# Where the low parts of stationary weights begin: one fixed place, or sixteen places in turn

## The chip, the cores and the metric

The kernel runs on one core of one Trainium2 chip. The metric is the device time of one execution in microseconds (us), as the median of several runs. The profile shows one execution, taken by the hardware profiler. Its engines are PE (TensorE, the matmuls), PEld (TensorE's weight loads), DVE (VectorE), ACT (ScalarE), POOL (GpSimd) and SP (SyncE, which issues most transfers).

## The reference

One decoder layer on 256 tokens of width 2048, in float32. A combined projection feeds a sliding-window attention (16 heads, learned sinks, ALiBi) and a forgetting attention (16 heads, per-head gates); both are normalised and sent through one output projection. Then comes a GeGLU channel mixer of width 5632 with a causal convolution of width 3 between the up-projection and the activation. Every sub-layer is `x + post_norm(f(pre_norm(x)))`:

```python
h = rmsnorm(x, pre_mix_g[l])
proj = h @ w_in[l]
...
mix = jnp.concatenate([o_a, o_b], axis=-1) @ w_out[l]
x = x + rmsnorm(mix, post_mix_g[l])
h = rmsnorm(x, pre_ffn_g[l])
u = causal_dwconv(h @ w_up[l], conv_w[l], conv_b[l])
gate, val = jnp.split(u, 2, axis=-1)
y = (jax.nn.gelu(gate, approximate=True) * val) @ w_down[l]
x = x + rmsnorm(y, post_ffn_g[l])
```

## The kernel before

**Split numbers.** Every matrix product is made of three products of a shorter float format (`float32r`): each operand is split into a high part, which is its rounded value, and a low part, which is the rest. The sum is high x high + high x low + low x high. The split of weights is `w_split` (lines 101 to 117): ScalarE writes the high part (line 111, tile `whi`), VectorE subtracts it from the raw weights and writes the low part (line 114, tile `wlo`). `w_high` (lines 89 to 99) does the same in two steps. A unit of weights is 128 partitions x 1024 numbers (512 KB), loaded by SyncE into `raw` (line 68), with five buffers each for `raw`, `whi` and `wlo`. The tile `wlo` is 128 numbers longer than a unit (line 85), so that a low part can begin later in it; the place is chosen in `w_parts` (lines 76 to 87).

**Two ways to multiply.** In `proj_T` (lines 242 to 269) and in `unit_T` (lines 213 to 240) the weights are the stationary operand, the one that is loaded into the array, and the activations `hT` are the moving operand. These calls hand `still=True` down to `w_parts`. `hT` holds the high part of the activations of 256 tokens in its columns 0 to 255 and the low part in columns 256 to 511, so one matmul of 512 columns with a high weight makes two of the three products (line 252), and one of 256 columns with a low weight makes the third (line 257). In `mm3` (lines 271 to 275), used by the value columns of the input projection, the output projection and the down-projection, activations are stationary and weights are the moving operand; there `still` is false and the low part begins at the start of its tile. `first_gate` (lines 841 to 881) uses `gate_unit` with `still=True` for one group of columns (matmuls at lines 860 and 864).

**Order on TensorE.** `proj_T` makes 256 columns of output from 2048 rows of weights, in two halves (`v` is 0 or 2) of two units each. A half is fifteen high matmuls, sixteen low ones in a row, and the last high one, in the order in which the code stands. Each of these matmuls has its own 128 columns of weights, so a weight load stands before each. TensorE's order is the program's own (line 46: `manual_schedule` for PE). Around the end of the mixer, ScalarE, VectorE and GpSimd have the program's order too (line 743); elsewhere a scheduler sets theirs. `tick` and `later` (lines 54 to 60) put steps of the attention between the matmuls of a projection.

**Stages in time.** Input projection and sliding-window attention come first, then the value columns, then the forgetting attention between further projections, then the output projection, then twice (for each half of the 5632 columns) the up-projection with `proj_T` and the down-projection with `mm3`.

**Memory.** Two unused tiles named `room` (lines 134 and 135) fill up the pools ahead of the others. In the built program the tiles `raw`, `whi`, `wlo`, `hT`, `rest`, `oT` and `G` all begin at multiples of 512 bytes in each partition.

Of the kernel before, what the change touches and what calls it, by code (L numbers as in the profile page):

```python
# [30 lines left out]
def hybrid_layer(ctx: ExitStack, tc: tile.TileContext, x, pre_mix_g, w_in, b_forget, sinks,  # L31
# [39 lines left out]
        return raw, a, c  # L71


    LOW = 80

    def w_parts(n, keep=None, still=False):


        if keep and keep[0] is None:
            return keep[1]  # L80
        if keep:
            return [keep[0].tile([P, UNIT], F32R, tag="h" + x, bufs=keep[1], name="w" + x)[:, :n]
                    for x in ("hi", "lo")]
        hi = wp.tile([P, UNIT], F32R, tag="whi", bufs=WB, name="whi")
        lo = wp.tile([P, UNIT + 128], F32R, tag="wlo", bufs=WB, name="wlo")
        c = LOW if still else 0
        return [hi[:, :n], lo[:, c:c + n]]

    def w_high(unit, keep=None, still=False):

        raw, a, c = unit
        n = a * c
        hi, lo = w_parts(n, keep, still)
        act.copy(hi, raw[:, :n])

        def low():
            dve.tensor_tensor(lo, raw[:, :n], hi.bitcast(F32), op=ALU.subtract)

        return [x.rearrange("p (a c) -> p a c", a=a) for x in (hi, lo)], low

    def w_split(unit, pin=False, keep=None, begun=None, between=None, still=False):

        raw, a, c = unit
        n = a * c
        hi, lo = begun or w_parts(n, keep, still)
        for i in range(2 if between else 1):
            cs = slice(i * 512, i * 512 + 512) if between else slice(0, n)
            if i:
                between()
            if not between or i:  # L110
                i1 = act.copy(hi[:, cs], raw[:, cs])  # L111
                if pin:
                    tc.keep_in_program_order(i1)
            i2 = dve.tensor_tensor(lo[:, cs], raw[:, cs], hi[:, cs].bitcast(F32), op=ALU.subtract)  # L114
            if pin:
                tc.keep_in_program_order(i2)
        return [x.rearrange("p (a c) -> p a c", a=a) for x in (hi, lo)]
# [163 lines left out]
    with tc.tile_pool(name="mixp", bufs=1) as mp:  # L281
# [47 lines left out]


        begun = w_parts(UNIT, still=True)
        tc.keep_in_program_order(dve.tensor_copy(begun[0][:, 0:512], head[:, 0:512]))
        x_part(0, (0,), "acc")
# [461 lines left out]
    with tc.tile_pool(name="ffn", bufs=1) as fp:  # L795
# [198 lines left out]
        for i, n in enumerate((512, 512, 512, 256, 256)):  # L994
            c = (0, 512, 1024, 1536, 1792)[i]
# [30 lines left out]
```

## Time and profile before

| | |
|---|---|
| median of 3 runs | 1082.71 us (1082.71 to 1083.7) |
| profiled execution | 1083.01 us, span 1081.2 us |
| granted TensorE clock | 0.997 |
| PE busy | 1069.4 us, 99% of the span, 6002 matmuls |
| PEld busy | 931.3 us, 86% |
| DVE busy | 735.1 us, 68% |
| ACT busy | 621.7 us, 57% |
| POOL busy | 186.1 us, 17% |
| memory read | 199.58 MB, 187 GB/s over the span |

The span goes from the first to the last instruction; the execution's time is a little longer. Rows of the profile name a line of the code, an engine, an operation, output and input tiles, and how often it occurs. Matmuls are pipelined: a row's duration of one matmul is longer than the distance from its start to the start of the next, so busy time does not tell how densely they follow. The distance is read from starts and counts in the timeline. In the chain of work that ended last, each piece is put down to the engine and line that the next one had to wait for.

### The profile page before, as it was taken

What the parts mean: (1) busy time and instruction counts of PE and PEld (TensorE: products, weight loads), DVE (VectorE), ACT (ScalarE), POOL (GpSimd) and SP (SyncE); (2) the same over time, 40 slices, a digit from 0 to 9 for tenths busy, and PEclk for the clock granted to TensorE, in tenths of its full rate; (3) what the DMA queues carried; (4) which work ended last, traced back from release to release, by engine and by line L of the source; (5) the groups of instructions that cost most, each with busy time, mean ns of one, the idle gap of its engine ahead of it and who ended that gap; (6) DMA issues with size and microseconds to landing.
All of it is one profiled execution on the core that took longest, in us unless ns stands there. A gap on an engine that the chain in (4) does not pass through costs nothing.

```text
span 1081.2 us, 16296 instructions
## 1 busy us (share of the span) xinstructions
PE 1069.4 (99%) x6002; PEld 931.3 (86%) x6002; DVE 735.1 (68%) x1193; ACT 621.7 (57%) x1069; POOL 186.1 (17%) x252
## 2 busy tenths in 40 slices
PE   9999999999999999999999999999999999999996
PEld 7889988888889888888888888888888888888886
DVE  5987877787467876777767444457777677765563
ACT  6766766667556765655556444456565565644450
POOL 4243334442022110101011000001010100101111
PEclk9999999999999999999999999999999999999998
DMA  8645556554863766566566556665665656665552
GB/s 284 205 132 162 175 159 203 167 165 156 291 234 105 233 191 195 182 192 196 184 191 191 194 196 192 195 197 178 192 195 189 190 187 193 189 196 192 192 167 78
DMA packets 164970, 202.88 MB, mean 188 GB/s; under 512 B 6780, under 2 KB 130972, under 8 KB 164380
## 3 DMA queue, kind: packets, MB, share of 16 engines
q1 hardware_dynamic: 164176, 201.27, 58.5%
q8 instruction: 47, 0.77, 0.3%
q10 hardware_dynamic: 716, 0.58, 0.2%
q14 instruction: 31, 0.25, 0.1%
HBM read 199.58 MB, written 2.11 MB: 187 GB/s over the span
## 4 chain that ended last, share of the span: by engine, by line
PE 94%; DVE 2%; POOL 1%; DMA 1%; ACT 1%; issue 0%; SPq 0%; DVEq 0%; POOLq 0%; ACTq 0%
PE bank_acc L275 35%; PE bank_acc L252 22%; PE bank_att L252 14%; PE bank_acc L257 11%; PE bank_att L257 7%; PE bank_att L440 1%; DVE wlo L114 1%; PE bank_att L484 1%; PE bank_att L475 1%; PE bank_att L486 0%; PE bank_att L220 0%; DMA cb<-c_dram 0%; DVE hT L721 0%; DMA x_in<-in_x_dram 0%; ACT whi L111 0%
## 5 line engine op out<-in xcount | busy, mean ns | idle before, releaser
L114 DVE TENSOR_TENSOR wlo<-raw,whi 128x1024 fp32r<-128x1024 f32 (+3 forms) x357 | 452.4, 1269 | 256.8 <-ACT whi L111 179.3
L111 ACT CAST whi<-raw 128x1024 fp32r<-128x1024 f32 (+3 forms) x356 | 368.1, 1036 | 187.4 <-PE bank_acc L275 119.7
L252 PE MATMUL bank_acc<-hT,whi 128*128 128x512 f32 x1088 | 266.6, 392 | 0.0
L252 PEld LDWEIGHTS bank_acc<-hT,whi 128*128 128x128 f32 x1088 | 198.3, 188 | 37.4
L275 PE MATMUL bank_acc<-whi,G 128*128 128x512 f32 (+1 forms) x724 | 214.4, 378 | 0.0
L275 PEld LDWEIGHTS bank_acc<-whi,G 128*128 128x128 f32 x724 | 133.7, 188 | 25.5
L252 PE MATMUL bank_att<-hT,whi 128*128 128x512 f32 x640 | 154.2, 391 | 0.0
L831 POOL TENSOR_TENSOR u<-u,rowf 128x256 f32<-128x256 f32 x88 | 54.4, 640 | 540.1 <-DVE u L830 537.8
L257 PEld LDWEIGHTS bank_acc<-hT,wlo 128*128 128x128 f32 x1088 | 138.5, 189 | 5.7
L257 PE MATMUL bank_acc<-hT,wlo 128*128 128x256 f32 x1088 | 142.2, 282 | 0.0
L252 PEld LDWEIGHTS bank_att<-hT,whi 128*128 128x128 f32 x640 | 117.6, 188 | 22.8
L275 PE MATMUL bank_acc<-wlo,G 128*128 128x512 f32 (+1 forms) x362 | 137.1, 379 | 0.0
L257 PEld LDWEIGHTS bank_att<-hT,wlo 128*128 128x128 f32 x640 | 81.0, 189 | 3.1
L275 PE MATMUL bank_acc<-whi,oT 128*128 128x512 f32 (+1 forms) x272 | 82.4, 380 | 0.0
L257 PE MATMUL bank_att<-hT,wlo 128*128 128x256 f32 x640 | 82.0, 281 | 0.0
L275 PEld LDWEIGHTS bank_acc<-wlo,G 128*128 128x128 f32 x362 | 68.1, 188 | 12.8
L275 PEld LDWEIGHTS bank_acc<-whi,oT 128*128 128x128 f32 x272 | 50.2, 188 | 9.3
L275 PE MATMUL bank_acc<-wlo,oT 128*128 128x512 f32 (+1 forms) x136 | 51.2, 377 | 0.0
L275 PE MATMUL bank_acc<-whi,hT 128*128 128x384 f32 (+1 forms) x192 | 47.5, 323 | 0.0
L829 ACT COPY cs<-bank_acc 128x256 f32<-128x256 f32 x48 | 15.9, 372 | 52.7 <-PE bank_acc L252 52.7
L458 ACT ACTIVATE p<-p,nm 128x256 f32<-128x256 f32 (+1 forms) x64 | 28.4, 444 | 27.7 <-DVE nm L446 27.7
L829 ACT COPY cs<-bank_att 128x256 f32<-128x256 f32 x40 | 13.3, 373 | 47.8 <-PE bank_att L252 47.6
(195 smaller groups left out, 1025.9 us busy)
## 6 DMA issues: line engine op xcount, KB each, us to landing
raw<-in_w_up_dram SPq DMA_DIRECT2D x176, 512.0 KB, 3.8
raw<-in_w_down_dram SPq DMA_DIRECT2D x88, 512.0 KB, 4.7
raw<-in_w_in_dram SPq DMA_DIRECT2D x51, 512.0 KB, 3.4
raw<-in_w_out_dram SPq DMA_DIRECT2D x32, 512.0 KB, 4.1
raw<-in_w_in_dram SPq DMA_DIRECT2D x16, 384.0 KB, 3.4
cb<-c_dram SPq DMA_DIRECT2D x8, 256.0 KB, 4.1
x_sb<-in_x_dram SPq DMA_DIRECT2D x2, 1024.0 KB
raw<-in_w_in_dram SPq DMA_DIRECT2D x5, 408.0 KB, 3.4
```

The source lines that it names most:

```text
L111: i1 = act.copy(hi[:, cs], raw[:, cs])
L114: i2 = dve.tensor_tensor(lo[:, cs], raw[:, cs], hi[:, cs].bitcast(F32), op=ALU.subtract)
L252: pe.matmul(b, parts[u][0][:, a, m * P:(m + 1) * P], hT[:, kt, :], start=(kt == 0), stop=(kt == KT - 1))
L257: pe.matmul(b[:, 256:512], parts[u][1][:, a, m * P:(m + 1) * P], hT[:, (v + u) * 4 + a, 0:256], start=False, stop=False)
L275: pe.matmul(b, a, r[:, cols], start=(first and i == 0), stop=(last and i == 2))
L440: pe.matmul(sb[e][:, cs], a[r, t * P:(t + 1) * P], b[r, 0:nk], start=(n == 0), stop=(n == 2))
L458: act.activation(p[:, e, cs], p[:, e, cs], AF.Exp, bias=nm[:, t, e:e + 1], scale=-1.0, accum_out=rs[:, t, e:e + 1])
L475: pe.transpose(pb[:, i * P:(i + 1) * P], p[:, e, c:c + P], ident)
L484: pe.matmul(ov, values(hl, 0), p[:, :, 0:256], start=(n == 0), stop=False)
L829: act.copy(c, b[:, 256:512])
L831: pool.tensor_tensor(u[:, 2:258], u[:, 2:258], rowf, op=ALU.mult)
```

## The change

The constant `LOW` goes. In its place a counter, `turn_no`, counts the units whose weights are stationary. The low part of such a unit begins at one of sixteen places in its tile, 8 numbers (32 bytes) apart; two units in succession share a place, then the place moves on by five sixteenths. The places in their order are 0, 40, 80, 120, 32, 72, 112, 24, 64, 104, 16, 56, 96, 8, 48 and 88 numbers, and then 0 again. Before, all these units began at 80 numbers. Since the counter is even at the start of each half of `proj_T`, both units of a half share a place. Units with weights as moving operand begin at 0 as before. The tile's size stays.

```diff
-    LOW = 80
+
+    turn_no = [0]
 
     def w_parts(n, keep=None, still=False):
...
         hi = wp.tile([P, UNIT], F32R, tag="whi", bufs=WB, name="whi")
         lo = wp.tile([P, UNIT + 128], F32R, tag="wlo", bufs=WB, name="wlo")
-        c = LOW if still else 0
+        c = turn_no[0] // 2 * 5 % 16 * 8 if still else 0
+        turn_no[0] += still
         return [hi[:, :n], lo[:, c:c + n]]
```

## The prediction

> **What bounds the kernel now.** I read the page first (busy time, then the chain that ended last), then the waits of TensorE, then its timeline and the durations by line, because the change moves no instruction.
>
> ```profile
> PE 1069.4 (99%) x6002; PEld 931.3 (86%) x6002; DVE 735.1 (68%) x1193; ACT 621.7 (57%) x1069; POOL 186.1 (17%) x252
> ...
> PE 94%; DVE 2%; POOL 1%; DMA 1%; ACT 1%; issue 0%; SPq 0%; DVEq 0%; POOLq 0%; ACTq 0%
> PE bank_acc L275 35%; PE bank_acc L252 22%; PE bank_att L252 14%; PE bank_acc L257 11%; PE bank_att L257 7%; PE bank_att L440 1%; DVE wlo L114 1%; PE bank_att L484 1%; PE bank_att L475 1%; PE bank_att L486 0%; PE bank_att L220 0%; DMA cb<-c_dram 0%; DVE hT L721 0%; DMA x_in<-in_x_dram 0%; ACT whi L111 0%
> ```
>
> TensorE is the bound: 94% of the chain is its own work. Line 257 is the pass with the moved operand, a low part as stationary operand: 11% + 7% = 18% of the chain, some 195 us. The waits of TensorE (engine, line, what for; us in total, times, longest) say that it waits for nearly nothing else:
>
> ```profile
> PE bank_acc L168 <- DVE junk L163: 1.3, 1, 1.3
> PE bank_att L630 <- POOL sqs L501: 0.9, 1, 0.9
> PE bank_acc L300 <- DMA x_in<-in_x_dram: 0.4, 1, 0.4
> PE bank_att L208 <- DVE diag L202: 0.4, 1, 0.4
> ```
>
> So the question is the rate at which the matmuls follow each other. The timeline of TensorE in the up-projection (start, length of the merged row, count at the end) shows it; one half of proj_T is one row of each kind:
>
> ```profile
> 463.86 2.05 PE L257 MATMUL bank_att<-hT,wlo 128*128 128x256 f32 x16
> 465.74 3.82 PE L252 MATMUL bank_att<-hT,whi 128*128 128x512 f32 x16
> 469.40 2.05 PE L257 MATMUL bank_att<-hT,wlo 128*128 128x256 f32 x16
> 471.28 3.82 PE L252 MATMUL bank_att<-hT,whi 128*128 128x512 f32 x16
> ```
>
> A row of x16 ends with the whole duration of its last matmul (0.28 us for a low, 0.39 for a high), so a low follows the low before it after (2.05 - 0.28) / 15 = 118.0 ns, and a high after (3.82 - 0.39) / 15 = 228.7 ns. Every load of weights stands between two of them. A matmul of 256 columns takes half of the time of one of 512, so behind a low there is the least time to load the next 128 columns, and a load that is held up shows at once. The same form, 256 columns with new weights each time, runs at two other rates in this trace:
>
> ```profile
> 176.93 1.30 PE L257 MATMUL bank_acc<-hT,wlo 128*128 128x256 f32 x10
> 190.75 1.30 PE L257 MATMUL bank_acc<-hT,wlo 128*128 128x256 f32 x10
> ...
> 1067.86 1.60 PE L275 MATMUL bank_acc<-rest,G 128*128 128x256 f32 x12
> 1069.30 0.28 PE L275 MATMUL bank_acc<-whi,G 128*128 128x256 f32 x1
> ```
>
> The two runs of line 257 in the attention stage go at (1.30 - 0.28) / 9 = 113.3 ns, at the place of today. At the end of the kernel, where the stationary operand is G, twelve go in 1069.30 - 1067.86 = 1.44 us, 120.0 ns each. The tiles of the built program tell the places: hT (and rest, in the same memory), whi, G and oT begin at multiples of 512 bytes; the low parts of proj_T begin 320 bytes past one (LOW = 80 elements), and every 128-column slice of them steps by 512, so the place is the same for all slices. Thus 120.0 ns stands for a place of 0 against a moving operand at 0, and 113.3 or 118.0 for 320 against 0. The modelled durations carry the same steps:
>
> ```profile
> L257 PE MATMUL bank_acc<-hT,wlo x1088: 276/281/386, 36.7 to 950.9; 128*128 128x256 f32 x182
> L257 PE MATMUL bank_att<-hT,wlo x640: 280/281/283, 369.7 to 928.8; 128*128 128x256 f32 x160
> L225 PE MATMUL bank_att<-hT,wlo x32: 280/281/416, 8.2 to 29.7; 128*128 128x256 f32 x32
> L225 PE MATMUL bank_acc<-hT,wlo x32: 276/280/287, 13.2 to 32.5; 128*128 128x256 f32 x32
> L860 PE MATMUL bank_acc<-hT,wlo x48: 223/276/281, 340.1 to 353.9; 128*128 128x128 f32 x32, 128*128 128x256 f32 x16
> L275 PE MATMUL bank_acc<-rest,G 128*128 128x256 f32 x24 | 3.2, 283 | 0.0
> ```
>
> 276 ns belongs to the runs at 113.3, 281 to those at 118, 283 (the last row, a mean) to those at 120. The longest, 287 at line 225, is 11 ns over 276: 113.3 + 11 = 124.3 ns is the slowest rate that the rows support.
>
> **The change, part by part.** Nothing is added or removed: every engine and queue has the same instructions in the same order with the same waits. What moves is the start of the low part: per pair of units it takes 0, 160, 320, 480, 128, 288, 448, 96, 256, 416, 64, 224, 384, 32, 192, 352 bytes and so on, instead of always 320. Of the rows above, 1088 + 640 (line 257) + 64 (line 225) + 48 (line 860) = 1840 matmuls load from it, 115 at each place on average.
>
> *Places that are multiples of 64 bytes* (eight of the sixteen, 920 matmuls). Two have rows: 320 goes at 118.0 ns and 0 at 120.0. For the other six nothing speaks for either end, so I take the middle for all eight, 119.0 ns: 920 x 1.0 ns = +0.9 us. Bounds, if all but 320 fell to one end: 113.3 ns, -4.3 us, and 124.3 ns, +5.8 us.
>
> *Places 32 bytes past a multiple of 64* (the other 920). No operand that TensorE reads here stands so; the trace has no row. The bounds are the same two rates, 113.3 and 124.3 ns, or -4.3 and +5.8 us. I take the middle of today's rate and the slow bound, (118.0 + 124.3) / 2 = 121.2 ns, near the 120.0 of place 0, because a start off the grid on which all else lies can make a load of 512 bytes touch one piece more and, on these rows, can hardly make it shorter than at 320: 920 x 3.2 ns = +2.9 us.
>
> *The high parts behind each run of lows.* Line 252 goes at 228.7 ns, while the same size at line 275 goes at 226.7, three matmuls in 1036.32 - 1035.64 = 0.68 us:
>
> ```profile
> 1035.64 0.61 PE L275 MATMUL bank_acc<-whi,G 128*128 128x512 f32 x2
> 1036.09 0.39 PE L275 MATMUL bank_acc<-wlo,G 128*128 128x512 f32 x1
> 1036.32 0.61 PE L275 MATMUL bank_acc<-whi,G 128*128 128x512 f32 x2
> ```
>
> That is 16 x 2.0 = 32 ns for each of 1728 / 16 = 108 halves, 3.5 us: the highs pay for some matmuls after the lows until loads and matmuls run in step again. A new place could end this (-3.5 us) or double it (+3.5). I take nothing, since both rates of the lows now lead into the same highs.
>
> *VectorE's subtraction (line 114, or 97), which writes the low part.* The same 228 tiles and bytes, only at another start. In the stretch from 370 to 560 us, which is up-projection alone:
>
> ```profile
> L114 DVE TENSOR_TENSOR wlo<-raw,whi 128x1024 fp32r<-128x1024 f32 x69 | 90.3, 1309 | 44.3 <-ACT whi L111 15.8 <-issue 13.8 <-PE bank_acc L257 7.3
> L111 ACT CAST whi<-raw 128x1024 fp32r<-128x1024 f32 x69 | 72.3, 1048 | 17.5 <-PE bank_att L252 9.1 <-PE bank_acc L252 8.4
> ```
>
> One of 1.31 us per unit lies under some 2.77 us of matmuls (half of 471.28 - 465.74), and VectorE sat idle 44.3 us before them in 190. A slowdown by a tenth would be 0.13 us of that; what hides it is VectorE's slack, and were it used up, line 257 would wait for wlo, which the waits of TensorE do not show now. I cost it at nothing. Loads from memory, ScalarE and the buffers' turns keep their order and sizes: nothing.
>
> *Sum*, against the profiled execution: 1083.01 (span 1081.2 and 1.8 around it) + 0.9 + 2.9 = 1086.8 us. The median of the runs is 1082.71, 0.3 below the profiled one; 1086.8 is 0.38% above it. About 0.2%, 2.2 us, is what a measurement of this kernel can tell from no change.
>
> **The rivals.** *Faster: most places are free.* One mechanism: whether a load meets the reads of the running matmul depends on the place, and 320, which is held up by 118.0 - 113.3 = 4.7 ns in nearly all its runs, is one of the bad ones. If 11 of 16 places ran at 113.3 and five at 120.0, the mean would be 115.4 ns, 1840 x -2.6 = -4.8 us, 1078.2 us. It needs more than 30% free places to break even (120.0 - 6.7 f = 118.0), and more than 48% for 0.2% (1.2 ns per matmul). For it: 113.3 occurs with the change's operands. Against: of two places with rows the other one is slower.
>
> *No change: the place does not set the rate.* The rows at 176.93 and 463.86 have one place and two rates, so the moment at which a run begins decides as well; G's 120.0 comes with another moving operand. If that were all, each place would show 118 mostly, and the time would be 1083.0 us. Against: about a hundred runs enter alike, in step, and go at 118.
>
> The Trainium skill has a rule that comes to the same: in "TensorE: Matmul & The Clock Gate", section "Step-by-step: what each phase is for", TensorE has two independent read ports, and loading the next tile's weights takes no read bandwidth from the running matmul. By that the place costs nothing, 1083.0 us; the rows at 113.3, 118.0 and 120.0 ns for one form do not bear it out fully.
>
> *Slower still: the odd places go at the slow bound.* If a start 32 bytes off the grid gave 124.3 ns, with the even ones at 119.0, it is 920 x 6.3 + 920 x 1.0 = +6.7 us, 1089.7 us. For it: all tiles lie on the grid. Against: 287 is the maximum of a row whose median is 280.
>
> **How the numbers follow.** My forecast, slower by about 3.8 us, gets 0.42; the slow bound at the odd places 0.20; no change 0.18; free places 0.20. So slower by over 0.2% is 0.62, within it 0.18, faster 0.20. The forecast's own range is 1084.5 to 1088.5 us (odd places between 118.5 and 123). For 8 in 10 the range reaches into the rivals of both signs, from 1080 to 1091 us: above lies the case of odd places at 124.3 with longer highs behind, below the larger half of the free case.
>
> **What would show it.** Right: the median duration of line 257 rises from 281 towards 283 or more, rows of x16 differ from half to half (above 2.05 us for the places 32 bytes off, the 2.08 of 120.0 ns or more at place 0), a pattern that repeats after sixteen halves; line 252 stays near 228.7 ns; no new wait of TensorE for wlo; line 114 keeps its 1.2 to 1.3 us. Wrong: rows of 1.98 us (113.3 ns) at many places, or all rows at 2.05 as now, or highs that move by more than 1 ns each.

## The result and the profile after

The changed kernel takes 1084.46 us (median of 14 runs, 1083.75 to 1085.82), the kernel before 1082.93 us on the same chip (14 runs, 1081.83 to 1083.7). The ratio is 1.0019, with a 95% interval of 1.0011 to 1.0026: slower by 1.5 us by the medians and 2.1 by the ratio, just under the 0.2% that a measurement can tell, though its interval leaves out no change. The forecast was +3.8 us. The measured median lies 0.04 us below the forecast's own range (1084.5 to 1088.5 us) and inside the range that was to hold in 8 of 10 cases (1080 to 1091 us).

Line 257 of before is line 259 here, line 252 is 254, line 114 is 116. First the waits of TensorE in the changed kernel (engine, line, what for; us in total, times, longest):

```profile
PE bank_acc L170 <- DVE junk L165: 1.3, 1, 1.3
PE bank_att L632 <- POOL sqs L503: 0.9, 1, 0.9
PE bank_att L210 <- DVE diag L204: 0.3, 1, 0.3
PE bank_att L222 <- ACT whi L113: 0.3, 1, 0.3
```

No wait for the low part of a half has come up. Neither has VectorE become slower; its subtraction in the stretch from 370 to 560 us:

```profile
L116 DVE TENSOR_TENSOR wlo<-raw,whi 128x1024 fp32r<-128x1024 f32 x69 | 90.3, 1309 | 45.0 <-ACT whi L113 16.1 <-issue 14.1 <-PE bank_att L259 7.4
```

1309 ns, as before to the nanosecond. The loss is inside the stream of matmuls. The timeline of TensorE in the up-projection shows it (start, length of the merged row, count), here the lows of eight halves in a row:

```profile
408.07 2.05 PE L259 MATMUL bank_acc<-hT,wlo 128*128 128x256 f32 x16
...
413.63 2.05 PE L259 MATMUL bank_att<-hT,wlo 128*128 128x256 f32 x16
415.52 3.85 PE L254 MATMUL bank_att<-hT,whi 128*128 128x512 f32 x16
419.21 2.04 PE L259 MATMUL bank_att<-hT,wlo 128*128 128x256 f32 x16
421.08 3.82 PE L254 MATMUL bank_att<-hT,whi 128*128 128x512 f32 x16
424.74 2.08 PE L259 MATMUL bank_att<-hT,wlo 128*128 128x256 f32 x16
...
430.32 2.08 PE L259 MATMUL bank_att<-hT,wlo 128*128 128x256 f32 x16
432.24 0.62 PE L254 MATMUL bank_att<-hT,whi 128*128 128x512 f32 x2
432.69 3.35 PE L254 MATMUL bank_acc<-hT,whi 128*128 128x512 f32 x14
435.88 2.05 PE L259 MATMUL bank_acc<-hT,wlo 128*128 128x256 f32 x16
...
441.43 2.03 PE L259 MATMUL bank_acc<-hT,wlo 128*128 128x256 f32 x16
...
446.96 2.08 PE L259 MATMUL bank_acc<-hT,wlo 128*128 128x256 f32 x16
```

Where all undisturbed halves of the up-projections took 2.05 us for sixteen lows before, they now take 2.03 to 2.08. By the code, the rows from 408.07 on begin at 288, 448, 96, 256, 416, 64, 224 and 384 bytes. The row at 415.52, highs behind place 448, is 3.85 us long where the others are 3.82: a place shows in the high parts too. The rows at 432.24 and 432.69 show how a half is made: fourteen high matmuls, sixteen low ones and two high ones (not fifteen and one, as the section on the kernel before has it). Where the bank does not change, the last two highs of a half and the first fourteen of the next stand in one row of sixteen.

The starts of the single matmuls in the trace give the cost of each place more finely. It repeats after 256 bytes: 320 costs what 64 does, 448 what 192 does, so there are eight different places. A half is undisturbed where no other matmul stands between its own, as in the up-projections; nearly all of these agree within a nanosecond for one place, though ScalarE, VectorE and the transfers do something else beside each.

| place modulo 256 | last high before the lows, ns | distance of lows, ns | last low and 15 highs behind, ns | sum of a half, ns |
|---|---|---|---|---|
| 0 | 226 | 119.5 | 3547 | 5566 |
| 32 | 235 | 118.3 | 3563 | 5573 |
| 64 (before: 320) | 226 | 117.8 | 3547 | 5540 |
| 96 | 229 | 117.3 | 3545 | 5534 |
| 128 | 233 | 120.4 | 3528 | 5567 |
| 160 | 237 | 119.7 | 3547 | 5580 |
| 192 | 226 | 117.8 | 3581 | 5574 |
| 224 | 235 | 116.8 | 3540 | 5527 |

Each time goes from the start of a matmul to the start of a later one. The sum is the first column, 15 distances of lows, and the third. Its mean is 5558 ns against 5540 ns for the one place of before: 18 ns for each of 108 halves, 1.9 us. The profiled executions agree, by the first and last start of line 257 or 259 (here the row of after; that of before is in the prediction):

```profile
L259 PE MATMUL bank_acc<-hT,wlo x1088: 274/281/388, 35.9 to 951.9; 128*128 128x256 f32 x182
```

From the first to the last low 951.9 - 35.9 = 916.0 us pass, before it was 950.9 - 36.7 = 914.2: 1.8 us more. The whole spans differ by only 1.0 us because this execution reached its first low 0.8 us earlier.

### The profile page after: what moved, and what is told of

The parts are those of the page before. It is cut to its first block, busy times and chain, and to the rows that moved or that the text cites. A ratio compares the mean times of both kernels' runs of the same rounds, so it can differ in the third digit from the quotient of the medians.

```text
span 1082.2 us, 16296 instructions
## 1 busy us (share of the span) xinstructions
PE 1070.2 (99%) x6002; PEld 930.3 (86%) x6002; DVE 735.5 (68%) x1193; ACT 622.0 (57%) x1069; POOL 185.8 (17%) x252
## 4 chain that ended last, share of the span: by engine, by line
PE 93%; DVE 2%; DMA 1%; POOL 1%; ACT 1%; issue 0%; SPq 0%; DVEq 0%; POOLq 0%; ACTq 0%
PE bank_acc L277 35%; PE bank_acc L254 22%; PE bank_att L254 14%; PE bank_acc L259 11%; PE bank_att L259 7%; PE bank_att L442 1%; PE bank_att L486 1%; PE bank_att L477 1%; DVE wlo L116 1%; DMA x_in<-in_x_dram 1%; PE bank_att L488 0%; DMA cb<-c_dram 0%; DVE hT L723 0%; POOL p L534 0%; ACT whi L113 0%
```

## The experiments

Theory 1: each place has a cost of its own, made of the last high before, the lows, and the highs behind, that does not depend on what the place before was. Theory 2, the rival: the places cost alike, and it is the change of place that costs. The first four kernels tell them apart; three keep one place throughout.

**One place, 56 numbers (224 bytes past a multiple of 256).**

```diff
-    LOW = 80
+    LOW = 56
```

> All low parts of stationary weights begin at 56 numbers (224 bytes past a multiple of 256). Theory 1, the costs of a place add up and repeat after 256 bytes: from the trace of the changed kernel, lows at 116.8 ns instead of 117.8 (15 x -1.0 = -15 ns a half), highs behind them 7 ns shorter, last high before the lows 9 ns longer: -13 ns for each of some 114 halves, 1.5 us faster than before. Theory 2, a place costs nothing and the change of place costs: the same as before within 0.3 us.

1081.9 us against 1083.11 before (11 and 23 runs); ratio 0.9990, interval 0.9981 to 0.9998: 1.1 to 1.2 us faster. It is the one kernel of this study with an interval wholly below the kernel before, though by less than 0.2%. A row of its timeline:

```profile
474.80 2.03 PE L257 MATMUL bank_att<-hT,wlo 128*128 128x256 f32 x16
```

2.03 us for sixteen lows, as at 441.43 in the changed kernel. The halves of its up-projections take 5525 to 5528 ns, where the table's sum is 5527.

**One place, 40 numbers (160 bytes).**

```diff
-    LOW = 80
+    LOW = 40
```

> All low parts begin at 40 numbers (160 bytes past a multiple of 256), the place with the longest sum in the changed kernel: lows 119.7 ns, highs as before, last high 10 ns longer. Theory 1: +40 ns a half, some 4.6 us slower than before, slower than the kernel with sixteen places. Theory 2: as before.

1087.15 us against 1083.11 (4 and 23 runs); ratio 1.0040, interval 1.0026 to 1.0054: 4.0 to 4.3 us slower, more than the kernel with sixteen places. Its halves take 5580 ns, the table's sum:

```profile
470.32 2.08 PE L257 MATMUL bank_att<-hT,wlo 128*128 128x256 f32 x16
```

**One place, 48 numbers (192 bytes).**

```diff
-    LOW = 80
+    LOW = 48
```

> All low parts begin at 48 numbers (192 bytes past a multiple of 256). In the changed kernel the lows of this place run at 117.8 ns, as those at 80 numbers do, and the highs behind them take 33 ns more. Theory 1: rows of sixteen lows as before, +34 ns a half in the highs, some 3.9 us slower than before. Theory 2, and also the view that the rate of the lows alone makes the difference: as before.

1086.51 us against 1083.11 (6 and 23 runs); ratio 1.0033, interval 1.0021 to 1.0045, though its lows go as before. Here are the first whole half, in the input projection, and one of the up-projections:

```profile
44.10 1.98 PE L257 MATMUL bank_acc<-hT,wlo 128*128 128x256 f32 x16
...
470.00 2.05 PE L257 MATMUL bank_att<-hT,wlo 128*128 128x256 f32 x16
471.89 3.85 PE L252 MATMUL bank_att<-hT,whi 128*128 128x512 f32 x16
```

In the up-projections the lows' rows are those of before, 2.05 us; the highs' row is 3.85 instead of 3.82, and a half takes 5573 or 5574 ns. So a place is paid for after its lows as well, and one that looks equal by the rate of line 257 costs 3.4 us. The row at 44.10 is an exception: at the same place, behind two highs that follow other work, its sixteen lows go at 113.3 ns.

**Turning between two places that are equal modulo 256.**

```diff
-        c = turn_no[0] // 2 * 5 % 16 * 8 if still else 0
+        c = (80, 16)[turn_no[0] // 2 % 2] if still else 0
```

> The place changes for every two units, but only between 80 and 16 numbers (320 and 64 bytes, both 64 past a multiple of 256). Theory 1: as before within 0.5 us, every half 5.54 us. Theory 2, the change of place costs: some 1.5 us slower, like the kernel with sixteen places.

1082.32 us against 1083.11; ratio 0.9998, interval 0.9989 to 1.0007. Turning by itself costs nothing that shows, and 64 and 320 are the same place: all undisturbed halves of the up-projections take 5539 or 5540 ns. Theory 2 falls with this and with fixed40 and fixed48, which never turn and are slower than the kernel that does.

**The two classes of the prediction's sum, each alone.** The prediction costed the multiples of 64 bytes and the places 32 past one apart.

```diff
-        c = turn_no[0] // 2 * 5 % 16 * 8 if still else 0
+        c = turn_no[0] // 2 * 5 % 8 * 16 if still else 0
```

> Only the eight places that are multiples of 64 bytes, in turn. The prediction's step: lows at 119.0 ns on average, all 1840 of them 1.0 ns over before, +1.8 us, and less than the odd places cost. Theory 1 with the costs by place read from the changed kernel's trace (5566, 5541, 5567 and 5574 ns a half for 0, 64, 128 and 192): +22 ns a half, some +2.5 us, more than the odd places cost.

```diff
-        c = turn_no[0] // 2 * 5 % 16 * 8 if still else 0
+        c = turn_no[0] // 2 * 5 % 8 * 16 + 8 if still else 0
```

> Only the eight places 32 bytes past a multiple of 64, in turn. The prediction's step: lows at 121.2 ns on average, 1840 x 3.2 ns, +5.9 us, three times what the even places cost. Theory 1 (5573, 5534, 5580 and 5527 ns a half for 32, 96, 160 and 224): +14 ns a half, some +1.5 us, less than the even places cost.

Even places: 1084.82 us against 1082.84, ratio 1.0019 (1.0010 to 1.0028). Odd places: 1084.73, ratio 1.0015 (1.0006 to 1.0024). The runs cannot tell the two apart, but the odd ones are far from the +5.9 us of the prediction's step; the even ones fit both its +1.8 and theory 1's +2.5. The mean halves in their traces are 5562 ns for the even and 5553 ns for the odd places, as the table's sums give.

Two runs ask what a place is measured from. Theory 3: from the moving operand, modulo 256. Theory 4: from the start of the memory, the load's place alone.

**Everything 64 bytes further on.**

```diff
-    const.tile([P, 120], F32, tag="room", name="room_c")
+    const.tile([P, 136], F32, tag="room", name="room_c")
```

> The unused tile ahead of all others is 64 bytes longer, so the moving operand hT, the high and the low parts all stand 64 bytes further on; the distances between them stay. Theory 3, what counts is the distance between the load's place and that of the moving operand modulo 256: halves of 5.54 us with lows at 117.8 ns as before. Theory 4, what counts is the load's own place: the low parts now stand at 128 past a multiple of 256, so lows at 120.4 ns as that place has in the kernel with sixteen.

1082.87 us beside 1082.65 for the kernel before, one run each. The halves take 5540 ns, and the lows 2.05 us a row as before, though they now stand at 128:

```profile
474.74 2.05 PE L257 MATMUL bank_att<-hT,wlo 128*128 128x256 f32 x16
```

**The moving operand alone 64 bytes further on.**

```diff
-    LOW = 80
+    LOW = 16
...
-        lo = wp.tile([P, UNIT + 128], F32R, tag="wlo", bufs=WB, name="wlo")
+        lo = wp.tile([P, UNIT + 64], F32R, tag="wlo", bufs=WB, name="wlo")
...
     x_in = main.tile([P, 2, D], F32, tag="x", name="x_in")
+    main.tile([P, 16], F32, tag="ahead", name="ahead")
...
     hT = main.tile([P, KT, 512], F32R, tag="hT", name="hT")
+    main.tile([P, 112], F32, tag="behind", name="behind")
```

> Only the moving operand hT stands 64 bytes further on; high parts stay at 0 and low parts at 64 past a multiple of 256 (16 numbers, in tiles of 1024 + 64 numbers). Theory 3: the lows get the distance 0 and run at 119.5 ns as place 0 does, the highs get a distance that the traces have not shown. Theory 4: lows at 117.8 ns and highs as before.

1087.01 us beside 1082.65, one run each. The lows have not moved modulo 256, and yet they run as place 0 did:

```profile
470.68 2.08 PE L259 MATMUL bank_att<-hT,wlo 128*128 128x256 f32 x16
472.59 3.84 PE L254 MATMUL bank_att<-hT,whi 128*128 128x512 f32 x16
...
741.29 2.08 PE L259 MATMUL bank_att<-hT,wlo 128*128 128x256 f32 x16
```

(2.08 - 0.28) / 15 = 120.0 ns. By the single starts there are two kinds of halves: in the first up-projection all forty undisturbed ones have lows at 120.0 ns and take 5593 or 5594 ns; in the second all forty-three have lows at 119.5 ns, just as place 0 had, and take 5573 or 5574. The addresses are the same in both; why the stream settles in two ways is open. (The whole time also holds the products of `mm3`, in which the shifted memory is an operand too.) Theory 4 falls with both runs; theory 3 stands for the lows. The cost thus depends on the load of the next weights and the reads of the running matmul together; how the two get in each other's way, the profile does not show. The Trainium skill, in "TensorE: Matmul & The Clock Gate", section "Step-by-step: what each phase is for", has these two on independent read ports, so that a load takes nothing from the running matmul. The runs do not bear that out: with the same instructions, and 3.7 us of waits listed for TensorE in each, the distance between the two addresses moves the kernel by 5.25 us (fixed56 to fixed40).

**Other places for the high parts.**

```diff
-        hi = wp.tile([P, UNIT], F32R, tag="whi", bufs=WB, name="whi")
-        lo = wp.tile([P, UNIT + 128], F32R, tag="wlo", bufs=WB, name="wlo")
-        c = turn_no[0] // 2 * 5 % 16 * 8 if still else 0
+        hi = wp.tile([P, UNIT + 64], F32R, tag="whi", bufs=WB, name="whi")
+        lo = wp.tile([P, UNIT + 64], F32R, tag="wlo", bufs=WB, name="wlo")
+        s = turn_no[0] // 2 - 28
+        d, c = (max(s, 0) // 10 % 8 * 8, (s % 10 - 2) % 8 * 8) if still else (0, 0)
         turn_no[0] += still
-        return [hi[:, :n], lo[:, c:c + n]]
+        return [hi[:, d:d + n], lo[:, c:c + n]]
```

> In the up-projections the high parts also change their place: eight places 32 bytes apart, each for ten halves in succession, while the low parts go through their eight places. It measures the sixty-four pairs. If the place of the high parts does not matter, every half has the sum that its low place had with high parts at 0, and no pair is below the 5.527 us of 224. If the step in which the highs run decides how the lows begin, the rate of one low place differs from one high place to the other, from 113.3 ns (a half of some 5.47 us) to 120.4.

1087.83 us beside 1082.65, one run each. From its timeline, highs at 0 (399.20) and at 64 bytes (488.94), a run of lows behind these (492.67), two halves of one pair of places (582.64 and 747.17, high parts at 128 and low parts at 192), and a half with high parts at 192 and low parts at 0 (825.59):

```profile
399.20 3.81 PE L255 MATMUL bank_acc<-hT,whi 128*128 128x512 f32 x16
...
488.94 3.89 PE L255 MATMUL bank_acc<-hT,whi 128*128 128x512 f32 x16
492.67 1.98 PE L260 MATMUL bank_acc<-hT,wlo 128*128 128x256 f32 x16
...
582.64 1.98 PE L260 MATMUL bank_acc<-hT,wlo 128*128 128x256 f32 x16
...
747.17 2.05 PE L260 MATMUL bank_att<-hT,wlo 128*128 128x256 f32 x16
...
825.59 2.08 PE L260 MATMUL bank_att<-hT,wlo 128*128 128x256 f32 x16
827.50 3.83 PE L255 MATMUL bank_att<-hT,whi 128*128 128x512 f32 x16
```

The highs at 0 go at (3.81 - 0.39) / 15 = 228.0 ns, at 64 at (3.89 - 0.39) / 15 = 233.3: the larger matmuls pay for a place as well. The row at 492.67 is a run of lows at (1.98 - 0.28) / 15 = 113.3 ns (113.7 by the single starts) with the low parts at 64, the place that goes at 117.8 behind highs at 0. So the highs before change how the lows run; but here the highs cost more than the lows gain. By the same sum as in the table no pair of places is below the 5527 ns of 224 behind highs at 0. Most pairs were seen in one half only.

Two more readings bear on the theories. The half at 825.59 has the distances of the run with the moved hT (192 from hT to the high parts, 0 to the low ones), with all three operands at other addresses; it takes 227 ns, lows at 119.5, 3554 ns and 5574 in all, which is what the second up-projection of that run takes. That is for theory 3. Against theory 1 as it was put: the two halves at 582.64 and 747.17 have the same pair of places and take 5529 and 5600 ns, lows at 113.3 and 117.8. They differ in what ran before them: low parts at 224 with high parts at 96, and low parts at 160 with high parts at 128. With the high parts at 0 the undisturbed halves repeat to a nanosecond; with the high parts elsewhere a pair has no single cost.

## Why the prediction was right or wrong

**Right: the bound and the direction.** TensorE did not come to wait for a low part, line 116 kept its time, and the stream of TensorE became longer, by 1.5 to 2.1 us instead of 3.8. Of the signs named, rows of lows that differ from half to half came; a median duration of line 257 rising from 281 did not (281 again), and 224, a place 32 past a multiple of 64, has rows below 2.05 us and not above.

**Right: the multiples of 64 bytes.** The prediction took 119.0 ns on average. The table's four are 119.5, 117.8, 120.4 and 117.8, a mean of 118.9; against the 117.8 of before that is 920 x 1.1 ns = 1.0 us where the prediction had 0.9. The middle was taken for want of a row on six of the eight places, so that it came out so closely is luck.

**Wrong in size: the places 32 bytes past a multiple of 64.** This is the step with the largest miss: it took 121.2 ns, +2.9 us, as the middle of today's rate and the slow bound, on the thought that a start off the grid can make a load touch one piece more. No run shows such a piece. The four measure 118.3, 117.3, 119.7 and 116.8 ns, a mean of 118.0: 920 x 0.2 ns = 0.2 us. Such a start is no class of its own; the fastest place of all, 224, is one of them. The thought that such a start could hardly be shorter than 320 was wrong: two of the four are. Nor did any place reach the slow bound of 124.3 ns, which came from one longest duration; the slowest goes at 120.4.

**Wrong in kind: the highs.** The step "The high parts behind each run of lows" took nothing, "since both rates of the lows now lead into the same highs". They do not. The last high before the lows, beside which the trace has the first load of the new place, takes 226 to 237 ns, and the last low and the highs behind it take 3528 to 3581. The picture itself was right: in the kernel before, behind the lows at 469.40, five highs take 229 to 235 ns and the rest 226 or 227. By the table's means the two add 5 + 3 = 8 ns to a half, 0.8 us: two thirds of what the lows add, and within the bound of 3.5 us that the prediction gave.

Together the lows' 1.2 us and the highs' 0.8 make 2.0 us, in place of 3.8.

**The rivals.** "Most places are free" did not happen: none of the eight places goes at 113.3 ns in the undisturbed halves. "The place does not set the rate" fell with the fixed places; but its ground, that the way in which a run begins also decides, is true: the scan shows lows at 113.3 ns behind highs that stand elsewhere. "Slower still" fell with the odd places.

**Too narrow: one reason.** The prediction held that a load shows behind the low matmul, because that leaves the least time for it. The highs, twice as long, pay too (233.3 ns against 228.0 in the scan). That speaks against a load that only comes too late, and for a running matmul that is drawn out itself; this is an argument and not shown, and which of the two gives way the runs do not tell.

## What to carry to other kernels

When TensorE is the bound and a stream of matmuls loads new weights each time, the distance between the addresses of stationary and moving operand, modulo 256 bytes, is a parameter worth a try; here it was worth up to 0.5% (1081.9 to 1087.15 us). Measure it by letting the place turn within one kernel and reading the trace place by place, then fix the best. Judge a place by the whole period of the stream, with the matmuls before and behind, not by the rate of the line that loads from it. Costs of places added up here to what fixed places then took, so one run served for all eight. That held with the high parts at distance 0 from hT; the scan and the moved hT show that it need not hold elsewhere, so the chosen place has to be run by itself.

## What was not expected of the hardware

The cost repeats after 256 bytes and, with the high parts at 0, is steady to a nanosecond: 5527 ns (224) to 5580 ns (160) for the same half of 32 matmuls, whatever the other engines did beside it. Moving everything by 64 bytes changed nothing (5540 ns), moving the moving operand alone by 64 changed a half to 5593 ns in one up-projection and to 5573 in the other. And a run of matmuls remembers how it was entered: at one place (192, high parts at 0) lows stay at 113.3 ns or at 117.8 for the whole run of sixteen, as at 44.10 and 470.00 us with the fixed place 48. Why a place costs what it costs stays open.
